# Block compression in a decoder layer: row-pair sums in place on VectorE and split a step later, a shorter GELU, weight splits at another spacing

## The chip, the cores and the metric

The kernel runs on one core of one Trainium2 chip. Its engines are TensorE (PE, and PEld for its weight loads), VectorE (DVE), ScalarE (ACT), GpSimd (POOL) and SyncE (SP), which issues most of the DMAs. The metric is the device time of one execution in microseconds, as the median of several runs; lower is better.

## The reference, cut to what matters

One decoder layer for a prompt of 256 tokens and for 8 sequences of 8 new tokens with 2048 cached tokens each: a SwiGLU block, a token mixer, a second SwiGLU block, each with a layer norm behind it. The mixer has a branch that compresses the cached keys and values. That is the part around the change:

```python
def compress(x, pos_emb, w1, w2):          # x: cached k or v, 16 tokens to a chunk
    chunks = x.reshape(B, n_chunks, CMP_STRIDE, NSA_KV_HEADS, NSA_HD)
    w1r = w1.reshape(2, CMP_STRIDE, NSA_HD, CMP_HIDDEN)
    h = einsum('pd,pdf->f', pos_emb, w1)
    for r in range(2):
        h = h + einsum('bnskd,sdf->bnkf', chunks, w1r[r])[:, r:r + n_cmp]
    return einsum('bnkf,fd->bnkd', gelu(h), w2)
```

Everything is float32. The kernel gets float32 precision from TensorE by splitting each operand into two numbers of a shorter type, a high part (a rounded copy) and a low part (the difference), and adding three products of parts.

## The kernel before

The program is written out in order: a Python generator emits one instruction stream per engine, each engine runs its stream in that order, and nothing is reordered afterwards. Background tasks (`spawn`) are woven in by a planner's clock: every matmul adds its estimated time to the clock, a task's `yield 2.5` means that its next part is emitted once 2.5 us more of matmuls have been emitted. So a yield decides beside which matmul an instruction stands, not when it runs.

The stages are: first SwiGLU, compression of the cache (`compress`), projections, attention, retention, output projection, second SwiGLU. Only the compression is touched.

**The compression** has 8 pairs (4 pairs of sequences for the keys, 4 for the values) and each pair 8 steps `m`, so 64 steps, and two halves `s2` in each step (`n` counts the 128 halves). In one half TensorE does three parts of six matmuls: two parts on even and odd rows (`eo`, weights `cw`) and a third on the sums of row pairs (`both`, weights `cs`). All are 128x128 by 128x256, 36 in a step. The operands of a step are made two steps ahead by `cx_split(m + 2)`: GpSimd adds the row pairs into two tiles `t` (L714), then ScalarE and VectorE split all rows (128x1024, into `r`) and the two sums (128x256 each, into `r` or `K`). `split` is L219 (ScalarE copies the high part) and L220 (VectorE subtracts it). Each buffer ring has three slots. The rows come in as 32 pages to a half of a pair by `cx_load` (L609); three rooms (`x0`, `x1`, `raw`) hold them in turn, and of each eight page loads SyncE issues six and GpSimd two.

When a pair's matmuls are done, `cpost` makes the output of the branch from them, twice (`f` 0 and 1): it puts the three accumulators together (L829 to L835), squares and adds the bias on ScalarE, runs `gelu` (L810, L811 on VectorE, the tanh on ScalarE at L813, L815 on VectorE), and then multiplies by `w2` on TensorE, at L208 into bank `m`. That product stands in TensorE's own stream between the matmuls of the next pair, so that TensorE waits there if L815 is late. After `f` 1, ScalarE copies the result to `y` (L852 or L855) and GpSimd stores it to `c_aside` (L858). From half 49 on, the weights of the value side are loaded and split while the key side is finished: `cw_split`, a half later the sum on GpSimd (`cw_sum`, L668) and `cs_split`.

Towards the end `x_scale` normalises the layer's input that was put aside, and `x_parts` splits it (L539, L540) for the first sweep of the projections. The tiles that it writes first lie in the memory where pair 6 keeps `y`, so they wait for pair 6's store to `c_aside`.

Of the kernel before, what the change touches and what calls it, by code (L numbers as in the profile page):

```python
# [11 lines left out]
AF = mybir.ActivationFunctionType  # L12
ALU = mybir.AluOpType
# [4 lines left out]
NT = 320  # L18
# [7 lines left out]
NTMP = 5  # L26
# [141 lines left out]
class Builder:  # L168
# [535 lines left out]

    def cx_split(self, m):
        half, j = divmod(m, 4)
        room = self.rooms[self.ROOMS[half]]
        x = room.rearrange("p (g a f) -> p g a f", g=32, a=4)[:, :, j]
        rows = x.rearrange("p g (s r c) -> p s r g c", s=2, r=2)
        eo, both = self.cx_ring(m)  # L710
        sums = []
        for s in range(2):
            t = self.t([128, NT], "t", bufs=NTMP)[:, 0:256]
            self.nc.gpsimd.tensor_tensor(t.rearrange("p (g c) -> p g c", c=8), rows[:, s, 0], rows[:, s, 1], op=ALU.add)  # L714
            sums.append(t)
        view = lambda t: t.rearrange("p (q g c) -> p g q c", q=4, c=8)
        self.split(view(eo[0]), view(eo[1]), x.rearrange("p g (q c) -> p g q c", c=8))
        for s in range(2):
            c = slice(256 * s, 256 * s + 256)
            self.split(both[0][:, c], both[1][:, c], sums[s])  # L720

    def compress(self):
# [7 lines left out]
        for n in range(128):  # L730
            m, s2 = divmod(n, 2)
            pair, i = divmod(m, 8)
            if s2 == 0:
                if n == 0:
                    self.rr_rest()
                if m < 62:
                    self.cx_split(m + 2)
                    self.rows_split = m == 61
                for load in loads.get(m, ()):
                    self.cx_load(*load)  # L740
# [29 lines left out]
            k, step = divmod(n - 49, 3)  # L770
            if 0 <= k < 8 and step == 0:

                self.cw_split(k, raw[k])
            elif 0 <= k < 8 and step == 1:
# [10 lines left out]
            if n == 114:  # L785
                self.w_limit, self.ahead = len(self.wq), 0
                self.w_feed()
# [19 lines left out]
    def gelu(self, hs, u, wait=0.0):  # L807

        nc = self.nc
        nc.vector.tensor_scalar(u, u, 0.044715, 1.0, op0=ALU.mult, op1=ALU.add)  # L810
        nc.vector.tensor_tensor(u, u, hs, op=ALU.mult)  # L811
        yield wait
        nc.scalar.activation(u, u, AF.Tanh, scale=math.sqrt(2.0 / math.pi))  # L813
# [3 lines left out]
    def cpost(self, pair, acc):  # L817
# [9 lines left out]
        for f in range(2):  # L827
# [16 lines left out]
            yield 2.5  # L844
# [920 lines left out]
    def first_splits(self, i):  # L1765
        self.cx_split(i)
        self.cs_split(i, self.sums_room(i))
# [117 lines left out]
```

## Time and profile before

| | us |
|---|---|
| median of 3 runs | 2862.51 |
| lowest, highest | 2862.44, 2864.89 |
| the profiled execution | 2862.96 |
| its span, first to last instruction | 2861.3 |
| TensorE busy in the span | 2786.0 (97%) |
| VectorE, ScalarE, GpSimd busy | 1580.3, 1210.4, 464.9 |
| compression: first matmul to the first of the projections | 947.48 to 1263.50 |

Times are microseconds from the span's start. A busy share of an engine is a mean over stages; the rows of the compression tell what each engine does there. Matmuls are pipelined: the distance of their starts is their cost, not the duration of one.

### The profile page before, as it was taken

To read this page: it belongs to the slowest core of one execution; us is meant where nothing else is said; L and a number is where in the kernel's file an instruction comes from. 1 tells how busy PE (TensorE), PEld (TensorE's weight loads), DVE (VectorE), ACT (ScalarE), POOL (GpSimd) and SP (SyncE) were. 2 spreads that over 40 slices of the span, in tenths; PEclk is the share of its full clock that TensorE was granted. 3 is DMA by queue.
4 is the path that set the end of the run, shared out by engine and by line. 5 is a ranking of instruction groups with operands and counts; after the bars stand their busy time and mean duration, and the time that the engine had idled before them with its cause. 6 is when DMAs were issued, how large, how long until landed. Compare 5 with 4: busy or idle time off the path is not lost. (4 is left out here: it accounts for less than half of the span.)

```text
span 2861.3 us, 49912 instructions
## 1 busy us (share of the span) xinstructions
PE 2786.0 (97%) x19841; PEld 2708.4 (95%) x19841; DVE 1580.3 (55%) x1939; ACT 1210.4 (42%) x1748; POOL 464.9 (16%) x548
## 2 busy tenths in 40 slices
PE   9999999999999998999999999999999999999996
PEld 8999999999999987998888888989999999999996
DVE  4333333347767878784574455673333333366665
ACT  4333333345445545554444445343333333354553
POOL 0000000000112656633232111450000000001111
PEclk9999999999999999999999999999999999999998
DMA  6555444455657444437677764544444444444442
GB/s 220 183 193 181 148 150 152 148 162 192 201 171 232 141 133 137 137 134 257 200 237 232 233 208 165 199 145 150 149 151 151 148 151 151 148 147 148 150 153 89
DMA packets 202603, 484.76 MB, mean 169 GB/s; under 512 B 24257, under 2 KB 100930, under 8 KB 200450
## 3 DMA queue, kind: packets, MB, share of 16 engines
q1 hardware_dynamic: 192546, 451.30, 49.1%
q0 software_dynamic: 9824, 30.29, 3.1%
q8 instruction: 155, 2.54, 0.4%
q14 instruction: 78, 0.64, 0.1%
HBM read 467.47 MB, written 22.28 MB: 171 GB/s over the span
## 5 line engine op out<-in xcount | busy, mean ns | idle before, releaser
L220 DVE TENSOR_TENSOR wl<-raw,wh 128x1024 fp32r<-128x1024 f32 x650 | 815.5, 1255 | 1066.4 <-ACT wh L219 1050.6
L219 ACT ACTIVATE wh<-raw 128x1024 fp32r<-128x1024 f32 x650 | 688.2, 1059 | 1153.2 <-PE m L214 1116.4
L213 PE MATMUL m<-x,wh 128*128 128x320 f32 x3664 | 1148.2, 313 | 9.1 <-ACT wh L219 6.5
L214 PE MATMUL m<-x,wh 128*128 128x320 f32 x3664 | 1132.4, 309 | 3.1 <-DVE x L540 3.1
L215 PE MATMUL m<-x,wl 128*128 128x320 f32 x3664 | 1132.0, 309 | 0.4 <-DVE wl L220 0.4
L213 PEld LDWEIGHTS m<-x,wh 128*128 128x128 f32 x3664 | 690.5, 188 | 32.3 <-issue 22.2
L214 PEld LDWEIGHTS m<-x,wh 128*128 128x128 f32 x3664 | 690.6, 188 | 5.1 <-DVE x L540 4.3
L215 PEld LDWEIGHTS m<-x,wl 128*128 128x128 f32 x3664 | 689.9, 188 | 0.8 <-DVE wl L220 0.8
L213 PE MATMUL m<-r,wh 128*128 128x320 f32 (+1 forms) x1592 | 495.4, 311 | 2.3 <-ACT wh L219 1.0
L215 PE MATMUL m<-r,wl 128*128 128x320 f32 (+1 forms) x1592 | 491.0, 308 | 0.0
L214 PE MATMUL m<-r,wh 128*128 128x320 f32 (+1 forms) x1592 | 487.8, 306 | 2.7 <-DVE r L220 2.7
L213 PEld LDWEIGHTS m<-r,wh 128*128 128x128 f32 x1592 | 298.8, 188 | 8.1 <-issue 3.7
L214 PEld LDWEIGHTS m<-r,wh 128*128 128x128 f32 x1592 | 299.3, 188 | 4.8 <-DVE r L220 3.9
L215 PEld LDWEIGHTS m<-r,wl 128*128 128x128 f32 x1592 | 298.5, 188 | 0.0
L476 POOL TENSOR_TENSOR t<-x,x 128x320 f32<-128x320 f32 x3 | 2.7, 916 | 1415.5 <-DVE x L456 719.6
L220 DVE TENSOR_TENSOR r<-G,r 128x640 fp32r<-128x640 f32 (+1 forms) x184 | 158.4, 865 | 0.0
L213 PE MATMUL x<-r,G 128*128 128x256 f32 x480 | 138.1, 288 | 0.0
L214 PE MATMUL x<-r,G 128*128 128x256 f32 x480 | 135.8, 283 | 1.4 <-DVE r L220 1.3
L215 PE MATMUL x<-r,G 128*128 128x256 f32 x480 | 135.1, 282 | 0.0
L219 ACT ACTIVATE r<-G 128x640 fp32r<-128x640 f32 (+1 forms) x184 | 130.1, 712 | 0.0
L214 PEld LDWEIGHTS x<-r,G 128*128 128x128 f32 x480 | 91.4, 190 | 3.4 <-DVE r L220 2.0
L213 PEld LDWEIGHTS x<-r,G 128*128 128x128 f32 x480 | 91.9, 192 | 1.4 <-issue 1.2
(389 smaller groups left out, 2390.3 us busy)
## 6 DMA issues: line engine op xcount, KB each, us to landing
raw<-wup SPq DMA_DIRECT2D x352, 512.0 KB
raw<-wdn SPq DMA_DIRECT2D x176, 512.0 KB
raw<-win_ret SPq DMA_DIRECT2D x48, 512.0 KB
raw<-win_nsa SPq DMA_DIRECT2D x40, 512.0 KB
raw<-wout SPq DMA_DIRECT2D x32, 512.0 KB
r<-pks SPq DMA_DIRECT2D x96, 128.0 KB
x<-pkc SPq DMA_DIRECT2D x152, 64.0 KB
K<-cw1k SPq DMA_DIRECT2D x16, 512.0 KB
```

The costliest lines, as they stand in the source:

```text
L213: mm(out, wh, xh, start=start, stop=False)
L214: mm(out, wh, xl, start=False, stop=False)
L215: mm(out, wl, xh, start=False, stop=stop)
L219: self.nc.scalar.activation(hi, src, AF.Copy)
L220: self.nc.vector.tensor_tensor(lo, src, hi.bitcast(F32), op=ALU.subtract)
L476: nc.gpsimd.tensor_tensor(s, self.d[0], self.d[1], op=ALU.add)
```

## The change

Four edits, all in the compression. Row pairs are no longer added by GpSimd into tiles of their own: VectorE adds both pairs in one instruction, in place in the room. Their split is one of 128x512 instead of two of 128x256 and is emitted one step later (`cx_both(m + 1)` beside `cx_split(m + 2)`). `gelu` has one VectorE instruction less: the first two are one. The weight splits of the value side stand 3.5 halves apart instead of 3, and the product with `w2` stands 5.0 planned us behind the GELU instead of 2.5 for pairs 0 to 6.

```diff
+    def cx_rows(self, m):
+        half, j = divmod(m, 4)
+        return self.rooms[self.ROOMS[half]].rearrange("p (g a f) -> p g a f", g=32, a=4)[:, :, j]
     def cx_split(self, m):
-        sums = []
-        for s in range(2):
-            t = self.t([128, NT], "t", bufs=NTMP)[:, 0:256]
-            self.nc.gpsimd.tensor_tensor(t.rearrange("p (g c) -> p g c", c=8), rows[:, s, 0], rows[:, s, 1], op=ALU.add)
-            sums.append(t)
+        x = self.cx_rows(m)
+        eo, _ = self.cx_ring(m)
         view = lambda t: t.rearrange("p (q g c) -> p g q c", q=4, c=8)
         self.split(view(eo[0]), view(eo[1]), x.rearrange("p g (q c) -> p g q c", c=8))
-        for s in range(2):
-            c = slice(256 * s, 256 * s + 256)
-            self.split(both[0][:, c], both[1][:, c], sums[s])
+        r = x.rearrange("p g (s r c) -> p g s r c", s=2, r=2)
+        self.nc.vector.tensor_tensor(r[:, :, :, 0], r[:, :, :, 0], r[:, :, :, 1], op=ALU.add)
+    def cx_both(self, m):
+        r = self.cx_rows(m).rearrange("p g (s r c) -> p g s r c", s=2, r=2)[:, :, :, 0]
+        _, both = self.cx_ring(m)
+        view = lambda t: t.rearrange("p (s g c) -> p g s c", s=2, c=8)
+        self.split(view(both[0]), view(both[1]), r)
...
                 if m < 62:
                     self.cx_split(m + 2)
-                    self.rows_split = m == 61
+                if m < 63:
+                    self.cx_both(m + 1)
+                    self.rows_split = m == 62
...
-            k, step = divmod(n - 49, 3)
-            if 0 <= k < 8 and step == 0:
+            k, step = divmod(2 * (n - 50), 7)
+            if 0 <= k < 8 and step in (0, 1):
                 self.cw_split(k, raw[k])
-            elif 0 <= k < 8 and step == 1:
+            elif 0 <= k < 8 and step in (2, 3):
...
-            if n == 114:
+            if n == 116:
                 self.w_limit, self.ahead = len(self.wq), 0
...
     def gelu(self, hs, u, wait=0.0):
-        nc.vector.tensor_scalar(u, u, 0.044715, 1.0, op0=ALU.mult, op1=ALU.add)
-        nc.vector.tensor_tensor(u, u, hs, op=ALU.mult)
+        nc.vector.scalar_tensor_tensor(u, u, 1.0 / 0.044715, hs, op0=ALU.add, op1=ALU.mult)
         yield wait
-        nc.scalar.activation(u, u, AF.Tanh, scale=math.sqrt(2.0 / math.pi))
+        nc.scalar.activation(u, u, AF.Tanh, scale=0.044715 * math.sqrt(2.0 / math.pi))
...
             yield from self.gelu(y, u, 1.5)
-            yield 2.5
+            yield 5.0 if pair < 7 else 2.5
...
     def first_splits(self, i):
         self.cx_split(i)
+        if i:
+            self.cx_both(0)
         self.cs_split(i, self.sums_room(i))
```

Two places show what moved. The first is VectorE's stream at the start of the compression, around the last four results of the first SwiGLU (L456). `r_856` and `r_867` (`r_865` after) are the rows of steps 0 and 1, `r_857` the sums of step 0, then of step 1, `wh` and `wl` hold weights. Before:

```order
L220 TENSOR_TENSOR r_856_8779<-x_791_7886,r_856_8779 128x32x4x8
L220 TENSOR_TENSOR r_857_8780<-t_8781,r_857_8780 128x256
L220 TENSOR_TENSOR r_857_8780<-t_8783,r_857_8780 128x256
L220 TENSOR_TENSOR wh_860_8791<-K_543_5515,wh_860_8791 128x512
L456 TENSOR_TENSOR x_587_5691<-x_587_5691,m_792_7887 128x320
L456 TENSOR_TENSOR x_589_5702<-x_589_5702,m_793_7894 128x320
L456 TENSOR_TENSOR x_591_5712<-x_591_5712,m_794_7901 128x320
L456 TENSOR_TENSOR x_593_5722<-x_593_5722,m_795_7908 128x320
L220 TENSOR_TENSOR r_867_8842<-x_791_7886,r_867_8842 128x32x4x8
L220 TENSOR_TENSOR r_857_8780<-t_8843,r_857_8780 128x256
```

After:

```order
L220 TENSOR_TENSOR r_856_8779<-x_791_7886,r_856_8779 128x32x4x8
L716 TENSOR_TENSOR x_791_7886<-x_791_7886 128x32x2x8
L220 TENSOR_TENSOR wh_858_8784<-K_543_5515,wh_858_8784 128x512
L456 TENSOR_TENSOR x_587_5691<-x_587_5691,m_792_7887 128x320
L456 TENSOR_TENSOR x_589_5702<-x_589_5702,m_793_7894 128x320
L456 TENSOR_TENSOR x_591_5712<-x_591_5712,m_794_7901 128x320
L456 TENSOR_TENSOR x_593_5722<-x_593_5722,m_795_7908 128x320
L220 TENSOR_TENSOR r_865_8835<-x_791_7886,r_865_8835 128x32x4x8
L716 TENSOR_TENSOR x_791_7886<-x_791_7886 128x32x2x8
L220 TENSOR_TENSOR r_857_8780<-x_791_7886,r_857_8780 128x32x2x8
```

L716 is the new sum in place. The split of step 0's sums, which stood ahead of the four results, now stands behind step 1's row split and sum.

The second is TensorE's stream where the compression ends: `x_1027` (`x_909` after) is the last accumulator of pair 7, `L208` the product of pair 6 with `w2`, and `m_1068` (`m_940` after) the first accumulator of the projections. Before:

```order
L214 MATMUL x_1026_13179<-r_856_8779,G_855_8752 128x256
L215 MATMUL x_1026_13179<-r_856_8779,G_855_8752 128x256
L213 MATMUL x_1027_13180<-r_857_8780,x_896_9287 128x256
L214 MATMUL x_1027_13180<-r_857_8780,x_896_9287 128x256
L215 MATMUL x_1027_13180<-r_857_8780,x_896_9287 128x256
L213 MATMUL x_1027_13180<-r_857_8780,x_896_9287 128x256
L214 MATMUL x_1027_13180<-r_857_8780,x_896_9287 128x256
L215 MATMUL x_1027_13180<-r_857_8780,x_896_9287 128x256
L213 MATMUL m_1068_13640<-x_1051_13560,wh_1042_13374 128x320
```

After:

```order
L214 MATMUL x_908_12870<-r_856_8779,G_855_8752 128x256
L215 MATMUL x_908_12870<-r_856_8779,G_855_8752 128x256
L208 MATMUL m_910_12878<-cw2v_384,x_872_8853 128x128 x4
L213 MATMUL x_909_12871<-r_857_8780,x_882_9250 128x256
L214 MATMUL x_909_12871<-r_857_8780,x_882_9250 128x256
L215 MATMUL x_909_12871<-r_857_8780,x_882_9250 128x256
L213 MATMUL x_909_12871<-r_857_8780,x_882_9250 128x256
L214 MATMUL x_909_12871<-r_857_8780,x_882_9250 128x256
L215 MATMUL x_909_12871<-r_857_8780,x_882_9250 128x256
L213 MATMUL m_940_13300<-x_932_13282,wh_917_13043 128x320
```

Pair 6's last product stands 6 matmuls ahead of the projections, where 54 matmuls stood between them before. In the same way every pair's first product stands 24 matmuls later than before, and every second one 48.

## Rows read from the trace of the kernel before

**Rows 1.** Page: busy us, share of the span and instructions of each engine.

```profile
PE 2786.0 (97%) x19841; PEld 2708.4 (95%) x19841; DVE 1580.3 (55%) x1939; ACT 1210.4 (42%) x1748; POOL 464.9 (16%) x548
```

**Rows 2.** Waits of PE, 947 to 1264: us in total, times, longest.

```profile
PE m L208 <- DVE x L815: 21.2, 6, 7.8
PE x L214 <- DVE r L220: 1.3, 2, 1.0
```

**Rows 3.** Timeline of PE: start, duration, instruction, [idle before <- releaser].

```profile
947.48 0.52 PE L213 MATMUL x<-r,G 128*128 128x256 f32 x1
...
1079.23 1.10 PE L208 MATMUL m<-x,cw2k 128*128 128x512 f32 x2 [1.83 <-DVE x L815]
...
1128.84 2.04 PE L208 MATMUL m<-x,cw2k 128*128 128x512 f32 x2 [7.78 <-DVE x L815]
...
1202.54 1.10 PE L208 MATMUL m<-cw2v,x 128*128 128x128 f32 x8
...
1238.04 1.09 PE L208 MATMUL m<-cw2v,x 128*128 128x128 f32 x8
...
1254.57 1.86 PE L208 MATMUL m<-cw2v,x 128*128 128x128 f32 x8 [2.21 <-DVE x L815]
...
1263.50 0.31 PE L213 MATMUL m<-x,wh 128*128 128x320 f32 x1
```

**Rows 4.** Windows: stretch, length, PE busy, granted clock, DMA share, GB/s.

```profile
1079.00:1083.00 4.00, 3.77 (x27) 1.00 0.19 56
...
1255.00:1259.00 4.00, 4.00 (x23) 0.59 0.36 103
```

**Rows 5.** Timeline of DVE, instructions beside which GpSimd added nothing.

```profile
948.87 1.23 DVE L220 TENSOR_TENSOR r<-x,r 128x1024 fp32r<-128x1024 f32 x1 [1.54 <-ACT r L219]
950.01 0.76 DVE L220 TENSOR_TENSOR r<-t,r 128x256 fp32r<-128x256 f32 x2
...
951.84 0.68 DVE L220 TENSOR_TENSOR wh<-K,wh 128x512 fp32r<-128x512 f32 x1
...
993.50 0.42 DVE L810 TENSOR_SCALAR x<-x 128x512 f32<-128x512 f32 x1
994.02 0.69 DVE L811 TENSOR_TENSOR x<-x 128x512 f32<-128x512 f32 x1
```

**Rows 6.** DVE by line and shape, 1057 to 1137: busy, mean ns of one.

```profile
L220 DVE TENSOR_TENSOR r<-t,r 128x256 fp32r<-128x256 f32 x18 | 15.1, 880 | 0.0
L220 DVE TENSOR_TENSOR r<-x,r 128x1024 fp32r<-128x1024 f32 x10 | 14.6, 1460 | 3.2 <-ACT r L219 3.2
L220 DVE TENSOR_TENSOR G<-K,G 128x1024 fp32r<-128x1024 f32 x8 | 11.0, 1381 | 3.4 <-ACT G L219 3.4
L220 DVE TENSOR_TENSOR K<-t,K 128x256 fp32r<-128x256 f32 x8 | 5.7, 750 | 0.0
L220 DVE TENSOR_TENSOR r<-raw,r 128x1024 fp32r<-128x1024 f32 x4 | 5.4, 1348 | 0.0
...
L220 DVE TENSOR_TENSOR wh<-K,wh 128x512 fp32r<-128x512 f32 x3 | 3.7, 1227 | 0.0
```

**Rows 7.** Timelines of POOL, ACT and PE: two sums; the late pages at 1018.

```profile
1134.84 1.43 POOL L714 TENSOR_TENSOR t<-x 128x256 f32<-128x256 f32 x2
...
1018.54 1.06 ACT L219 ACTIVATE r<-x 128x1024 fp32r<-128x1024 f32 x1 [9.63 <-DMA x<-pkc]
...
1021.16 0.39 PE L214 MATMUL x<-r,G 128*128 128x256 f32 x1 [0.39 <-DVE r L220]
```

**Rows 8.** Timelines of ACT, POOL and DVE at the end of the compression.

```profile
1256.47 0.60 ACT L855 ACTIVATE x<-m 128x512 f32<-128x512 f32 x1 [4.54 <-PE m L208]
...
1257.37 0.57 POOL L858 DMA_DIRECT2D c_aside<-x  x1 [12.92 <-ACT x L855]
...
1260.87 1.02 ACT L539 ACTIVATE x<-x,vecs 128x320 fp32r<-128x320 f32 x2 [3.80 <-DMA c_aside<-x]
...
1261.47 0.55 DVE L540 SCALAR_TENSOR_TENSOR x<-x,vecs,x 128x320 fp32r<-128x320 f32 x1 [4.49 <-ACT x L539]
```

More of the change, by code (lines that the diff above doesn't have):

```diff
@@ L703, in cx_ring @@
             [self.rb[m % 3][:, 512 * k:512 * k + 512] for k in range(2)]
+    def cx_rows(self, m):
+        half, j = divmod(m, 4)
+        return self.rooms[self.ROOMS[half]].rearrange("p (g a f) -> p g a f", g=32, a=4)[:, :, j]
     def cx_split(self, m):
[L706 to L710, printed above, removed]
-        sums = []
-        for s in range(2):
-            t = self.t([128, NT], "t", bufs=NTMP)[:, 0:256]
-            self.nc.gpsimd.tensor_tensor(t.rearrange("p (g c) -> p g c", c=8), rows[:, s, 0], rows[:, s, 1], op=ALU.add)
-            sums.append(t)
+        x = self.cx_rows(m)
+        eo, _ = self.cx_ring(m)
         view = lambda t: t.rearrange("p (q g c) -> p g q c", q=4, c=8)
         self.split(view(eo[0]), view(eo[1]), x.rearrange("p g (q c) -> p g q c", c=8))
-        for s in range(2):
-            c = slice(256 * s, 256 * s + 256)
-            self.split(both[0][:, c], both[1][:, c], sums[s])
+        r = x.rearrange("p g (s r c) -> p g s r c", s=2, r=2)
[5 more added lines that the diff above has]
+        self.split(view(both[0]), view(both[1]), r)
     def compress(self):
```

## Prediction

> **What bounds the kernel now.** I read the page's busy shares first: TensorE is busy for 97% of the span, the next engine, VectorE, for 55% [rows 1]. Over the whole span only TensorE can be the bound, so a change to other engines is worth what TensorE waits for in the stage that is touched. The waits of TensorE in the compression are next: 21.2 us in six waits of the `w2` product for L815, the last VectorE instruction of GELU, and 1.3 us for row splits [rows 2]. The starts of these products then give a ruler. Between 1202.54 and 1238.04 nothing waits: a pair of 8 steps costs 35.5 us, a step 4.44 us and one matmul 35.5 us less two products, over 288, about 0.117 us [rows 3]. Eight such pairs from 947.48 would end at 1231.5. The first matmul of the projections starts at 1263.50 [rows 3], so the stage holds 32 us that are not matmuls. 22.5 of them are the waits; most of the rest is the low clock behind the waits: after the one of 2.21 us the granted clock was 0.59 of 2.4 GHz (a stretch partly at its 1.2 GHz level) for 4 us, which costs 1.6 us, after the one of 1.83 us it stayed at 1.00 [rows 3, 4]. These **32 us are all that the change can win**.
>
> Why is L815 late? In the crowded stretch from 1057 to 1137, where weights are split as well, a step's rows cost VectorE 14.6 + 5.4 us in 14 instructions and the sums 15.1 + 5.7 us in 26, that is 1.43 + 2 x 0.80 = 3.03 us [rows 6]. Without GpSimd beside it the same work takes 1.23 + 0.76 = 1.99 us [rows 5]. So 1.04 us in a step is paid for the two sums that GpSimd makes at the same time; they take it 1.43 us [rows 7].
>
> **The change part by part.**
>
> *The sums move to VectorE.* Per step GpSimd loses two sums, VectorE gains one of 128x512. No such instruction is in the trace. From below it is bounded by a plain two-operand instruction of this size, 0.69 us, from above by one of this size with GpSimd beside it, 1.23 us [rows 5, 6]; I take 0.69, since GpSimd now adds only for the weights. The split is one of 0.68 us instead of two of 0.38 [rows 5]. A step's rows are then 1.23 + 0.69 + 0.68 + 0.1 for the sum's wait for the split in front of it (L811 starts 0.52 us behind L810, which lasts 0.42 [rows 5]) = 2.7 us: 0.3 us less than the crowded 3.03, but 0.7 more than the quiet 1.99. VectorE is not relieved much; it becomes independent of GpSimd.
>
> The Trainium skill (SBUF — State Buffer, section Who interferes with whom) says that a VectorE instruction with two SBUF inputs and a GpSimd instruction that reads SBUF exclude each other for their whole length. By that rule the two sums would have cost VectorE up to 1.43 us a step where the rows say 1.04, and the crowded stretch would lose 0.4 us x 18 steps = 7 us more of VectorE work than I count; the stalls that I leave there below would then be nil. The trace agrees in kind and is smaller in size; the sum goes by the rows.
>
> *GELU loses an instruction* of 0.42 us [rows 5], and its product with `w2` stands 24 (f 0) or 48 (f 1) matmuls later, 2.8 or 5.6 us. The shown waits: 1.83 goes with that alone; 7.78 needs 5 us more, and TensorE's own wait and VectorE's contention in front of L815 supply most of it; the 2.21 at the end goes too. I leave 1 us, which also covers pair 7, whose products stand 12 matmuls, 1.4 us, earlier. Bounds: 0, and 5 with the clock.
>
> *The sums are split a step later.* This is what the change costs, since TensorE's third part now follows its operands by one step less. In a quiet step they are ready in time: ScalarE 1.06 and, by size, 0.6, VectorE 2.7 us against a step of 4.44 plus two parts, 1.5 us. Three places are not quiet:
> - *Start.* The sums of step 0 were split ahead of 947; now they follow step 1's rows. VectorE starts these at 948.87 [rows 5]; 1.23 + 0.1 + 0.69 + 0.6 later the low part is there, at 951.4. TensorE wants it 13 matmuls behind 947.48, at 949.1. Cost 2.3 us; bounds 0 and 3.9 with the clock.
> - *Late pages at 1018.* ScalarE waits 9.63 us for pages until 1018.54, TensorE today only 0.39 us, because it lives on two finished steps [rows 7]. SyncE's page issues set that time, and they do not change. Now the sums of step 15 queue behind step 16's rows: 1.1 us of ScalarE, then 1.15 + 0.1 + 0.69 + 0.6 of VectorE, ready at 1022.2. Step 16's second matmul was due at 1020.8 [rows 7], and step 15's third part needs its low operand 24 matmuls ahead of that, at 1018.0, plus 1.4 us: the start's stall less the other 0.9 us of row waits, which go [rows 2, 7]. Cost 2.8, with 1 for the clock 3.8; bounds 1 and 5.
> - *The end.* `x_scale` and the last rows share VectorE; rows and GELU leave it 1 us a step, and no row prices the rest. I take half of the wait of 2.21 us that stands there now [rows 3], 1.2; bounds 0 and 4.
>
> *Crowded stretch.* The rows 2.7, the weights (1.23 + 0.68 quiet) / 1.75 steps = 1.1, and GELU with what stands before it, six instructions of 0.4 to 0.7 us twice in a pair less the 0.42 [rows 5], 0.7 a step: 4.5 us, less 0.08 for each start that overlaps the end in front of it, so about 4.1 against 4.44. GpSimd's weight sums still collide, and ScalarE still waits for them in its order. I keep 2.5 us for 14 steps; bounds 0 and 10 (the weights at the contended 1.38 and 1.23 of [rows 6], the sum's row at 0.9).
>
> *The store of pair 6.* The first sweep's operands may be written only when pair 6's result has been stored. Today the product starts at 1254.57, ScalarE copies it at 1256.47, GpSimd issues the store at 1257.37, ScalarE splits the first operand at 1260.87 and VectorE at 1261.47 [rows 3, 8]. That chain is 6.9 us long, 7.4 with VectorE's half, and 54 matmuls, 6.3 us, hid it: the projections start at 1263.50 without a wait. At full clock the product takes 1.1 instead of 1.86 us [rows 3], so the chain is 6.1 and 6.7 us. Now 6 matmuls stand between, and TensorE is through them 1.6 us after the product's start. **It waits some 5 us there**, 5.4 with the second operand, and pays 1.6 for the clock: 7.0 us. Bounds: 3 if the store lands faster, 9.
>
> *Nothing for:* the later weight release (n 116), since the first weights arrive ahead of the sweep; the spacing 3.5, counted above.
>
> Sum: 2.3 + 3.8 + 2.5 + 1.2 + 7.0 + 1 = 17.8 us of new stalls against 32 us that go. **14 us are left.** Its own time of the profiled execution is 2862.96 us, 1.7 more than the span and 0.45 above the median 2862.51, so 2862.5 - 13.5 to 14 gives 2849.
>
> **The rivals.**
> - *The small margins hold:* no stall at the start or in the crowded stretch, the store lands in 2 us. New stalls 8 us, time 2838 to 2841. For it: 0.6 us of the 4.44 are free. Against it: the wait at the store is plain in the order. Chance 0.18.
> - *The waits only move:* VectorE stays full in the crowded stretch, and what the `w2` product waited, the third part now waits, 10 us with the clock, and the late pages cost 5. New stalls 27 us, time 2857 to 2862. For it: 4.1 of 4.44 leaves little, and the bound above is 10. Chance 0.17.
> - *The edit does not do what it says:* the products still wait as now, since L815's lateness comes from ScalarE's order and not from VectorE. Then 10 of 22 us stay and 7 are added: 2858. Chance 0.04.
> - *VectorE becomes the bound of every step (slower):* the sum in place and its split read runs of 8 with gaps. At 1.23 us each they make 1.23 + 1.23 + 1.23 + 0.1, 3.8 us, with 0.7 of GELU 4.5 in every step; it decides from 4.44 on. In the 14 crowded steps 5.6 us, 16 us of stalls, elsewhere 0.1 x 50 = 5; with the 17.8 less 2.5, 36 us against 32: 2867, and 2890 if the row splits are dear too. Against it: the row split reads and writes such runs now, at 1.23 us for 1024, as much as a plain one. Chance 0.06.
>
> **How the numbers follow.** The forecast, 2849 (2843 to 2855), has 0.55; the others sum to 0.45. The range 2838 to 2862 holds the first rival, the forecast and the moved waits, and leaves out the slower case and the corners. What a measurement of this kernel can tell from no change is about 0.2%, 5.7 us: faster means below 2856.8. Faster: 0.55 + 0.18 + 0.03 of the moved waits = 0.76. Same: the rest of the moved waits and the fourth case, 0.16. Slower 0.08, where 0.02 stands for stalls at the store beyond my bound.
>
> **What would show it.** In the changed profile: no wait of the `w2` product above 2 us; a wait of 2 us of a third part for VectorE right behind the first matmuls, and one of about 3 near 1020; 4 to 6 us of idle TensorE between the last compression matmul and the first of the projections, ended by ScalarE's L539 and behind it the store to `c_aside`; L716 near 0.69 us; GpSimd busy about 100 us less. The forecast is wrong if L716 or the 128x512 split lasts over 1 us, if third parts wait in most steps, or if the projections start without a wait.

## The result and the profile after

| | before | changed |
|---|---|---|
| median, us | 2863.7 (4 runs beside the changed kernel) | 2882.3 (4 runs, 2879.4 to 2884.2) |
| profiled execution, its span | 2862.96, 2861.3 | 2884.2, 2882.5 |

The changed kernel is **slower**, by a ratio of 1.0054 (95% interval 1.0042 to 1.0066): 18.6 us between the medians, 12 to 19 us by the interval, where 14 us of gain were forecast. The page after, against [rows 1]:

```profile
span 2882.5 us, 49616 instructions
PE 2797.6 (97%) x19841; PEld 2715.4 (94%) x19841; DVE 1553.5 (54%) x1921; ACT 1202.3 (42%) x1684; POOL 346.5 (12%) x420
```

GpSimd is 118 us less busy and VectorE 27 us, as the edits mean it. Now TensorE's waits in the compression (us in total, times, longest), against [rows 2]:

```profile
PE m L214 <- DVE r L220: 10.1, 10, 2.8
PE m L214 <- DVE K L220: 4.5, 6, 1.7
PE m L213 <- ACT x L219: 3.4, 1, 3.4
PE x L214 <- DVE r L220: 2.5, 1, 2.5
PE m L213 <- ACT r L219: 2.4, 2, 1.3
```

No wait of the product with `w2` is left, and in their place third parts (into bank `m`, in pair 7 into `x`) wait for a split, 20 times in these rows. Single ones in TensorE's timeline of the changed kernel (start, us, line, what the idle time in brackets ended with), against [rows 3]: the start of the stage, pair 4's last step, a quiet pair, the first sweep of the projections, pair 7's product, and a later product that waits for a transfer.

```profile
951.66 0.48 PE L214 MATMUL m<-r,wh 128*128 128x256 f32 x1 [1.69 <-DVE r L220]
...
1151.32 0.39 PE L213 MATMUL m<-r,x 128*128 128x256 f32 x1 [3.38 <-ACT x L219]
...
1185.44 0.39 PE L214 MATMUL m<-r,K 128*128 128x256 f32 x1 [0.15 <-DVE r L220]
...
1274.67 0.42 PE L213 MATMUL m<-x,wh 128*128 128x320 f32 x1 [3.28 <-ACT x L539]
1275.69 0.41 PE L214 MATMUL m<-x,wh 128*128 128x320 f32 x1 [0.61 <-DVE x L540]
...
1317.50 0.74 PE L208 MATMUL x<-cw2v,r 128*128 128x128 f32 x4 [1.69 <-DVE r L819]
...
1329.90 0.67 PE L208 MATMUL x<-G,G 128*32 128x256 f32 x8 [1.66 <-DMA G<-cw1k]
```

The best reading is a ruler that counts work and not waits. The compression has 2304 matmuls beside the `w2` products, 288 to a pair. The table has the time from each pair's first matmul to the next one's (pair 7's to the first matmul of the projections), read from TensorE's timeline by counting. A pair without a wait takes 35.5 us; pair 0 has no product in it. The labels e1 to e18 are the experiments below; e15 to e17 also have the edge copy of e6 and the early product of e5.

| pair | 0 | 1 | 2 | 3 | 4 | 5 | 6 | 7 | sum |
|---|---|---|---|---|---|---|---|---|---|
| before | 37.4 | 35.6 | 42.6 | 43.4 | 46.2 | 35.7 | 35.5 | 39.6 | 316.0 |
| changed | 41.4 | 37.3 | 37.2 | 43.7 | 50.0 | 36.9 | 36.8 | 43.7 | 327.0 |
| e1 sums split at once | 38.9 | 43.4 | 39.5 | 52.0 | 58.9 | 40.0 | 38.5 | 48.0 | 359.2 |
| e2 sums on GpSimd, a step later | 41.2 | 39.4 | 35.5 | 46.1 | 51.1 | 35.7 | 35.6 | 41.4 | 326.0 |
| e3 changed, sums ahead of rows | 38.4 | 40.7 | 36.8 | 42.8 | 50.9 | 35.7 | 35.6 | 45.1 | 326.0 |
| e4 before, GELU and later product | 37.4 | 41.2 | 36.7 | 46.1 | 45.8 | 35.7 | 36.0 | 39.9 | 318.8 |
| e10 before, fixed pages | 37.5 | 35.5 | 36.1 | 43.5 | 46.2 | 36.6 | 35.5 | 38.1 | 308.9 |
| e13 before, no sums | 36.1 | 35.7 | 36.8 | 37.4 | 42.7 | 35.7 | 35.5 | 35.6 | 295.5 |
| e14 before, no weights | 37.4 | 35.7 | 43.1 | 35.4 | 35.4 | 35.7 | 35.5 | 38.2 | 296.4 |
| e17 new weights' order, rows first | 39.9 | 43.4 | 37.0 | 41.8 | 45.0 | 36.7 | 37.0 | 40.7 | 321.5 |
| e15 the same, sums ahead | 38.4 | 40.6 | 36.9 | 40.7 | 42.9 | 35.7 | 35.6 | 40.1 | 311.0 |
| e16 the same, early product | 38.4 | 35.4 | 37.8 | 39.1 | 44.2 | 35.7 | 35.5 | 36.3 | 302.4 |
| e18 without the new weights' order | 38.4 | 35.6 | 38.3 | 39.3 | 44.8 | 35.7 | 35.5 | 36.3 | 303.8 |

Of the 21.2 us between the two spans, 11 lie in the compression, 7.6 between the first sweep and the first product with the selected pages (147.4 us before, 155.0 after), and 2.4 behind it, less than the 4.8 us by which the changed kernel's own runs differ. The compression's loss is in pairs 0, 3 and 4, 5 and 6 and 7; pairs 1 and 2 gain 3.7 us. Eight pairs of 35.5 us would be 284: of the changed kernel's 43 us above that, 28.4 are idle time of TensorE (22.6 of 32 before), and the rest are matmuls at a slower pace behind waits, in part at a granted clock of 0.60 of 2.4 GHz (952 to 956) and 0.57 (1098 to 1102), stretches partly at the 1.2 GHz level.

What bounds pairs 3 and 4? Two windows, before and changed, over these pairs (bounds, length, then busy us of TensorE, its loads, VectorE, ScalarE, GpSimd, then granted clock and DMA):

```profile
1063.00:1153.00 90.00, 75.64 (x590) 71.64 (x589) 77.85 (x90) 50.67 (x87) 61.95 (x76) 0.94 0.46 134
```

```profile
1064.00:1157.00 93.00, 78.24 (x581) 73.35 (x581) 67.26 (x84) 47.46 (x71) 30.54 (x42) 0.94 0.47 136
```

VectorE fell from 86% busy to 72%, and the stretch became longer. No engine is full in it. What ScalarE and then VectorE wait for there, in the changed kernel:

```profile
ACT x L836 <- DVE x L835: 11.0, 4, 4.2
ACT wl L219 <- POOL K L668: 9.2, 3, 4.1
ACT wh L219 <- POOL K L668: 7.8, 3, 3.0
ACT x L219 <- POOL K L668: 5.0, 1, 5.0
```

```profile
DVE r L220 <- ACT r L219: 7.4, 9, 2.2
DVE G L220 <- ACT G L219: 5.7, 4, 2.6
DVE wl L220 <- ACT wl L219: 4.0, 2, 2.1
```

Each engine stands in its own order behind a wait for another one. What TensorE feels of that depends on the **lead** of its operands. I took, for each step, the start of its first matmul less the end of VectorE's row split for it. Before, the lead is 6.2 to 7.6 us in pair 6 and sinks to 1.9 at step 30 and -0.3 at step 35, and TensorE does not wait for rows there. In the changed kernel it never sinks under 4.1 and stands at 4.1 to 4.3 at twelve steps, 3, 6, 15, 23, 30, 35, 37, 47, 55, 58, 59 and 63: about a step (36 matmuls, 4.2 us) is now the least it can be, since the sums of step m queue behind the rows of step m+1, and TensorE must stop for them first. So late rows show as waits of the third part, a step earlier.

### The profile page after: what moved, and what is told of

Same layout as the page of the kernel before. It is cut to its first block, busy times and chain, and to the rows that moved or that the text cites. A ratio compares the mean times of both kernels' runs of the same rounds, so it can differ in the third digit from the quotient of the medians.

```text
span 2882.5 us, 49616 instructions
## 1 busy us (share of the span) xinstructions
PE 2797.6 (97%) x19841; PEld 2715.4 (94%) x19841; DVE 1553.5 (54%) x1921; ACT 1202.3 (42%) x1684; POOL 346.5 (12%) x420
## 5 line engine op out<-in xcount | busy, mean ns | idle before, releaser
L213 PEld LDWEIGHTS m<-x,wh 128*128 128x128 f32 x3664 | 692.0, 189 | 36.1 <-issue 22.6
L220 DVE TENSOR_TENSOR r<-x,r 128x1024 fp32r<-128x1024 f32 (+1 forms) x76 | 75.7, 996 | 40.3 <-ACT r L219 40.3
L213 PEld LDWEIGHTS x<-r,G 128*128 128x128 f32 x480 | 92.4, 192 | 1.1 <-issue 1.0
```

The costliest lines, as they stand in the source:

```text
L213: mm(out, wh, xh, start=start, stop=False)
L220: self.nc.vector.tensor_tensor(lo, src, hi.bitcast(F32), op=ALU.subtract)
```

## The experiments

All ratios are to runs of the kernel before on the same chip, with 95% intervals. Theory 1 was that the loss is the third part's lead, given up by the late split; its rival that VectorE's load, with the sum in it, makes everything late.

**e1: the split at once.**

```diff
                 if m < 62:
                     self.cx_split(m + 2)
-                if m < 63:
-                    self.cx_both(m + 1)
+                    self.cx_both(m + 2)
```

> The changed kernel with one thing undone: the sums in place are split at once, behind the row split of the same step (as the kernel before did), not a step later. VectorE still makes the sums. Theory 1 (the delay: the third part follows its operands by one step too little, and every lateness of VectorE or ScalarE now reaches TensorE): the 24 us of third-part waits between 947 and 1263 in the changed kernel go, the stall at pair 6's store and what follows it stay; 2852 to 2858. Theory 2 (VectorE's load: the sum of 0.69 to 1.0 us in its queue makes rows and GELU late, wherever the split stands): no more than a quarter of the waits goes; 2876 to 2884, with waits of first and second parts in place of third ones.

2910.6 us, 1.0156 (1.0139 to 1.0173): slower still. Neither theory had this. ScalarE's waits from 947 to 1063:

```profile
ACT r L219 <- DVE x L716: 20.7, 10, 2.1
ACT K L219 <- DVE x L716: 10.6, 5, 2.3
ACT r L219 <- DVE raw L716: 10.3, 5, 2.1
ACT K L219 <- DVE raw L716: 8.7, 3, 4.6
```

Directly behind the rows' high part ScalarE comes to the sums' high part, for which VectorE has first to finish the rows' low part and the sum: 50 us in 23 waits, as many as VectorE makes sums in that stretch, with all else on ScalarE queued behind. With the sum on VectorE some distance is needed; e3 and e15 show that it can be less than the changed kernel's.

**e2 and e3: whose load, which order.** e2 puts the sums back on GpSimd and leaves their split a step later:

```diff
-        self.nc.vector.tensor_tensor(r[:, :, :, 0], r[:, :, :, 0], r[:, :, :, 1], op=ALU.add)
+            self.nc.gpsimd.tensor_tensor(t..., rows[:, s, 0], rows[:, s, 1], op=ALU.add)
+            self.pair_sums[m % 3].append(t)
...
+            self.split(both[0][:, c], both[1][:, c], self.pair_sums[m % 3][s])
```

e3 exchanges two calls in the changed kernel:

```diff
-                if m < 62:
-                    self.cx_split(m + 2)
                 if m < 63:
                     self.cx_both(m + 1)
                     self.rows_split = m == 62
+                if m < 62:
+                    self.cx_split(m + 2)
```

> The changed kernel with the sums back on GpSimd (into tiles t, as before), but still split a step later, as two splits of 128x256. Theory 1 (the delay): third parts wait as in the changed kernel, 2876 to 2890, since ScalarE and VectorE still reach the sums behind the next step's rows. Theory 2 (VectorE's load): the third-part waits go with the sum, 2852 to 2862.

> The changed kernel with the order inside a step turned: the sums of step m+1 are split ahead of the rows of step m+2, not behind them. No instruction more or less. Theory 1 (the delay, by way of the queue: the sums wait in ScalarE's and VectorE's order behind 1.06 + 1.23 + 0.69 us of the next rows, and behind the pages that these wait for): most third-part waits and the start's go, rows have the slack, 2856 to 2866. Theory 2 (VectorE's load): the order changes nothing in the load, 2876 to 2886.

e2: 2879.1 us, 1.0044 (1.0027 to 1.0061); third parts wait as in the changed kernel, without any sum on VectorE. That speaks for theory 1. e3: 2875.9 us, 1.0035 (1.0022 to 1.0047), 5 to 6 us less than the changed kernel by ratio and median: the quiet pairs are mended and pair 0 in part (its first wait of 1.68 us stays), but pairs 1, 3 and 4 are not. Pairs 3 and 4 take 93.7 us in both. So the lead is a part of the loss only, and not, by itself, the loss of the crowded pairs.

**e4: the two edits that were to win, alone.** The kernel before with the shorter GELU and

```diff
-            yield 2.5
+            yield 5.0 if pair < 6 else 2.5
```

> The kernel before with only the shorter GELU and the later product with w2 (5.0 planned us instead of 2.5), for pairs 0 to 5. Sums on GpSimd, split at once, spacing 3. If the 22 us of w2 waits are lost only because the product stands too early: they go and nothing takes their place, as the third part keeps its two steps of slack: 2840 to 2846, waits of third parts under 2 us in sum. Rival (the waits only move: VectorE's lateness in the crowded stretch reaches the row splits instead): first or third parts wait 10 us or more, 2852 to 2860.

2867.4 us, 1.0008 (0.9997 to 1.0018): **nothing is won**, though no lead was given up for it. The waits of TensorE in the compression, and two rows of ScalarE's timeline:

```profile
PE m L208 <- DVE x L814: 18.3, 8, 4.5
PE x L214 <- DVE r L220: 3.1, 3, 1.2
```

```profile
1012.14 0.63 ACT L812 ACTIVATE x<-x 128x512 f32<-128x512 f32 x1 [1.95 <-DVE x L810]
1017.08 1.06 ACT L219 ACTIVATE r<-x 128x1024 fp32r<-128x1024 f32 x1 [4.31 <-DMA x<-pkc]
```

The product stands 24 or 48 matmuls later and waits 18.3 us in eight pieces, not 21.2 in six. `f` 1's GELU starts after `f` 0's product, so it moves with it; pair 0's second one came to wait 4.1 us behind the late pages of step 16. Pairs 1 and 2 are 77.9 us long (78.2 before), pairs 3 and 4 91.9 (89.6). The waits only moved, with the sums and their lead left alone. What they are the end of was the next question.

**e5: pair 6's product early** in the changed kernel.

```diff
-            yield 5.0 if pair < 7 else 2.5
+            yield 5.0 if pair < 6 else 2.5
```

> The changed kernel, but pair 6's product with w2 stands as early as before (2.5 planned us; the others stay at 5.0). Theory 1 (the store of pair 6 behind its late product holds the projections, and the low clock and the late start of pair 7 follow from it): the waits of 3.3 and 0.6 us at the first sweep go, the stage to the projections ends 5 to 6 us earlier and what is lost behind it shrinks too: 2872 to 2877. Theory 2 (the stall only moves to the product itself, since GELU of pair 6 is late anyway behind x_scale's VectorE work): a wait of 2 us or more at that product instead, 2878 to 2884.

2873.6 us, 1.0032 (1.0021 to 1.0044): 8.8 us less than the changed kernel by the medians, 6.3 by the ratios. The waits of 3.28 and 0.61 us at the first sweep shrink to 0.24 and 0.17, as the first theory had it. In the two profiles only some 2 us of the gain lie ahead of the first sweep, the rest behind.

**e6, e7, e8, e9: ScalarE's and GpSimd's waits.** e6 (before) and e8 (changed) put the small copy that ScalarE waits at (L832, L836) ahead of VectorE's sum. e7 and e9 are e6 with the weights' order changed: in e7 the split of the weights' sums stands half a step behind GpSimd's L668, in e9 L668 itself stands half a step later too, and the split behind that. The edge copy, and e9's weights:

```diff
             nc.scalar.activation(u[:, 0:256], q, AF.Copy)
+            nc.scalar.activation(rows[:, 1, 127:128], two(p[:, 254:256]), AF.Copy)
             yield 1.0
             nc.vector.tensor_tensor(rows[:, 1, 0:127], ...)
-            nc.scalar.activation(rows[:, 1, 127:128], two(p[:, 254:256]), AF.Copy)
...
+            if 0 < k < 9 and step == 0:
+                self.cs_split(k - 1, ...)
-            elif 0 <= k < 8 and step == 1:
-                self.cw_sum(place, r)
-                self.cs_split(k, place)
+            elif 0 <= k < 8 and step == 2:
+                self.cw_sum(..., raw[k])
```

> The kernel before with two lines exchanged: the small copy of the last column (L832, 128x2, ScalarE) stands directly behind the copy L829, ahead of VectorE's L831, and not behind it. Theory 3 (ScalarE stands in its order behind this copy, 22 us between 947 and 1160, with the rows' high parts queued behind it, so the length of the crowded pairs is a chain of ScalarE and VectorE waiting for each other and no engine's load): rows and tanh come earlier, the w2 waits fall by a third or more; 2850 to 2858. Rival (VectorE's load: it is busy for 78 of 90 us between 1063 and 1153): ScalarE's time there is idle anyway and the w2 waits stay; 2860 to 2867.

> As the one before, and the split of the weights' sums stands a half step behind GpSimd's sum, not directly behind it, so that ScalarE does not stand waiting for L668 (18 us between 1063 and 1160 in the kernel before). Theory 3: pairs 3 and 4, now 89.6 us long, shorten to 76 to 82; with the copy 2840 to 2852. Rival (VectorE's load): they stay at 87 to 92 us, 2858 to 2867.

> The changed kernel with the same two lines exchanged (its L835 and L836). Theory 3: ScalarE's 20 us at this copy go, rows reach the floor of the third part's slack less often; 2866 to 2876. Rival (VectorE's load, or the slack of the third part alone): 2878 to 2884.

> The kernel before with the two lines of the edge copy exchanged and the weight work of the value side pulled apart: GpSimd's sum L668 stands two half steps behind the weight split that it must wait for (one before), the split of these sums one half step behind it. Theory 3 (in the crowded pairs three engines stand in their order behind each other: VectorE's weight split, GpSimd's L668, GpSimd's row sums L714 behind it, ScalarE and VectorE behind those): GpSimd's 23 us of waits for VectorE in front of L668 go, and pairs 3 and 4 shorten from 89.6 to 75 to 82 us; 2844 to 2854. Rival (VectorE's own work, 78 of 90 us busy, sets them): 86 to 90 us, 2858 to 2866.

e6 2861.2 us, 0.9988 (0.9978 to 0.9997); e7 2862.7, 0.9987 (0.9977 to 0.9996); e8 2878.5, 1.0048 (1.0031 to 1.0064); e9 2862.9, 0.9996 (0.9987 to 1.0006). 3 or 4 us at most (e6), e8 not to be told from the changed kernel, and no more for taking GpSimd's waits away: theory 3 (engines that wait for each other in their orders, and no engine's load), as I had it, fell for the kernel before. In e9 VectorE is busy for 79 of the 86 us of pairs 3 and 4 and hardly waits; that its load, with GpSimd's sums beside it, is then the next limit is my reading, which e13 supports and no run isolates.

**e10: pages from fixed places** in the kernel before.

```diff
-                queue.dma_start(out=out, in_=self.I[name][bass.ds(v, 1)]...)
+                queue.dma_start(out=out, in_=self.I[name][(a + k + i) % 160][:, part])
```

> The kernel before, but the cached keys and values are taken from fixed pages and not from those in the page table (so the compression's input is another, and the reading of the table is left out); as many transfers of the same size by the same queues. SyncE issues pages almost without a pause from 960 to 1045 in the kernel before, 0.67 us each. Theory 4 (the page issues set when pair 2's rows come, and the w2 wait of 4.7 us at 1035 is ScalarE's wait for pages): an issue takes 0.35 to 0.45 us, ScalarE's wait of 9.6 us goes, pairs 0 to 2, now 115.6 us, shorten to 108 to 110, 2855 to 2859. Rival (the pages are early enough, GELU is late by itself): pair 2 stays at 42 us and the time at 2862 to 2866.

2859.7 us, 0.9985 (0.9975 to 0.9994), and pair 2 falls from 42.6 to 36.1 us. Of SyncE's timeline 24 page issues of the kernel before, then of e10:

```profile
984.04 15.86 SPq L609 DMA_DIRECT2D raw<-pkc  x24
```

```profile
979.81 11.24 SPq L607 DMA_DIRECT2D raw<-pkc  x24
```

And of TensorE's timeline pair 1's first product, in the kernel before, then in e10:

```profile
1040.12 1.19 PE L208 MATMUL m<-x,cw2k 128*128 128x512 f32 x1 [4.66 <-DVE x L815]
```

```profile
1034.96 0.67 PE L208 MATMUL m<-x,cw2k 128*128 128x512 f32 x1 [0.30 <-DVE x L819]
```

An issue takes 0.47 us in place of a mean of 0.66, pages come earlier, and the wait of 4.66 us "for L815" is gone. It was a wait for pages, by way of ScalarE's order.

**e11, e12: the spacing and the queue** in the changed kernel: weights 3 half steps apart; four of eight page loads on GpSimd in place of two.

```diff
-            k, step = divmod(2 * (n - 50), 7)
+            k, step = divmod(n - 49, 3)
```

```diff
-            self.pages(..., 2 if half > 1 else 0)
+            self.pages(..., 4 if half > 1 else 0)
```

> The changed kernel with the weight splits 3 half steps apart, as before. If the wider spacing costs (the last weight sum is needed at step 39, and TensorE waits 3.4 us there for its split): pair 4 falls from 50.0 to 45 or 46 us, 2876 to 2879. Rival (it is what keeps VectorE from being overrun, as the change means it): third parts wait more in pair 3, 2883 to 2890.

> The changed kernel, but GpSimd issues four of each eight page loads (two in the changed one): it has lost the row sums, 100 us of work, and SyncE is full from 960 to 1045. Theory 4 (SyncE's issues limit pairs 0 to 2): the third-part waits near 1018 and 1055 to 1060, 2.5 us with the clock's part 4, go; 2877 to 2880. Rival (the slack of the third part is short for its own reasons): 2881 to 2884.

e11: 2879.9 us, 1.0050 (1.0033 to 1.0067), not to be told from the changed kernel by the time; in the profile the wait of 3.4 us for the last weights at 1151.32 goes and pair 4 is 47.6 us long. e12: 2890.0 us, 1.0092 (1.0075 to 1.0109). My reading was wrong: GpSimd, in its order, now waits for rooms to come free with the weights' sums behind it, and ScalarE waits 6.1 us for one of these and 12.0 for three others (3.7 and 9.2 in the changed kernel). That accounts for a part of the loss only; pair 0 alone grew by 3.9 us, and I did not follow that up.

**e13, e14: without the sums, without the weights** in the kernel before.

```diff
-            self.nc.gpsimd.tensor_tensor(t..., rows[:, s, 0], rows[:, s, 1], op=ALU.add)
-            sums.append(t)
+            sums.append(rows[:, s, 0])
```

```diff
-            if 0 <= k < 8 and step == 0:
-                self.cw_split(k, raw[k])
-            elif 0 <= k < 8 and step == 1:
-                ...
```

> The kernel before with GpSimd's row sums left out: the third part is split straight from the first row of each pair (so its numbers are not the sums). Splits, their places and all else stay. It shows the most that taking the sums off GpSimd could win, as VectorE gets no sum in their place. If GpSimd's sums are what makes VectorE late in pairs 3 and 4 (its rows and splits are a third longer beside them): VectorE's busy time there falls from 78 to 60 us, the pairs from 89.6 to 76 to 80, the w2 waits of pairs 2 to 4 go, 2847 to 2853, with pair 2's wait for pages left. Rival (the weights' chain between ScalarE, VectorE and GpSimd sets the pairs): 85 to 90 us, 2858 to 2864.

> The kernel before with the value side's weights left out: no load, split or sum of them, the value side runs on the key side's weights (so its numbers are others). It shows what the weights cost in pairs 3 and 4. If these pairs are long only by the weight work: 71.5 to 73 us in place of 89.6, and only pair 2's wait for pages is left; 2844 to 2848. Rival (the row work alone already fills VectorE beside GpSimd's sums): 78 us or more, 2852 to 2858.

e13: 2849.6 us, 0.9942 (0.9925 to 0.9958); e14: 2848.7 us, 0.9942 (0.9926 to 0.9959). Pairs 3 and 4 take 80.1 us without the sums, 70.8 without the weights. So in the kernel before the weights make these pairs long; row work beside GpSimd's sums alone fits. The windows of e13 and e14 over the pairs:

```profile
1055.00:1135.00 80.00, 73.44 (x586) 70.40 (x585) 60.29 (x88) 49.65 (x87) 31.66 (x42) 0.96 0.55 158
```

```profile
1064.00:1135.00 71.00, 71.00 (x588) 69.08 (x588) 55.84 (x74) 38.83 (x71) 44.32 (x68) 1.00 0.44 125
```

VectorE's 77.85 us become 60.29, for the same splits and GELU work: 17.6 us in 16 steps are paid for GpSimd's sums. The sums' removal is worth 9.5 us there and 5.8 in pair 2, where the rows catch up faster once the pages are there; e13 keeps ScalarE's wait of 10.8 us for them.

**e15 to e18: can the change's idea win?** e15 is the changed kernel with the sums' split ahead of the rows (e3), pair 6's product early (e5), the edge copy first (e8) and the weights 3 half steps apart in the order of e9. e17 is e15 with the rows first again; e16 is e15 with all products at 2.5; e18 is e16 without the edge copy and the weights' order of e9. e18 against the changed kernel, beside e3's exchange:

```diff
-            yield 5.0 if pair < 7 else 2.5
+            yield 2.5
...
-            k, step = divmod(2 * (n - 50), 7)
+            k, step = divmod(n - 49, 3)
```

> The changed kernel with four things done otherwise: the sums of step m+1 split ahead of the rows of step m+2, pair 6's product early, the edge copy first, and the weights 3 half steps apart with GpSimd's sum two and its split three half steps behind the weight split. All work is done. If VectorE's shorter load (67 us in place of 78 in pairs 3 and 4) can be used once the third part's slack and the engines' orders are mended: pairs 3 and 4 take 78 to 84 us, no third part waits over 1.5 us, 2850 to 2858. Rival (the split behind the sum in place costs the slack anyway): 90 us or more, 2864 to 2872.

> As e15, but the product with w2 stands at 2.5 planned us in all pairs, as in the kernel before: of the changed kernel's four edits the later product is gone too. If the later product is of no use once VectorE is less busy (and in pair 1 harms, since GELU of pair 0 then queues behind the late pages: 3.5 us wait there in e15): pair 1 falls from 40.6 to 36 us and part of it returns in pair 2, 2851 to 2857. Rival (the later product is what keeps pairs 3 and 4 at 83.6 us): w2 waits there rise by 5 us or more, 2860 to 2866.

> As e15, but with the changed kernel's order inside a step: the sums of step m+1 split behind the rows of step m+2. It shows what the split's place alone costs. If the third part's lost slack is the main loss of the changed kernel: third parts wait 10 us or more again, pairs 5 and 6 take 36.8 in place of 35.7 us, 2866 to 2872. Rival (the weights' order and pair 6's product were the loss, and the place of the split is worth little): 2857 to 2861.

> The changed kernel with the sums in place and the shorter GELU, but the sums of step m+1 split ahead of the rows of step m+2, the product with w2 at 2.5 planned us everywhere and the weights 3 half steps apart; the edge copy and the weights' order as in the kernel before. If these three are enough (e16 without its edge copy and its weights pulled apart): 2853 to 2858, pairs 3 and 4 at 84 to 87 us. Rival (GpSimd's and ScalarE's waits at the weights hold the freed VectorE back, so that the sums alone gain nothing): pairs 3 and 4 at 90 us or more, 2860 to 2867.

| | us | ratio to before | interval |
|---|---|---|---|
| e15 | 2857.6 | 0.9968 | 0.9956 to 0.9981 |
| e17 | 2866.1 | 0.9999 | 0.9990 to 1.0008 |
| e16 | 2851.9 | 0.9949 | 0.9936 to 0.9963 |
| e18 | 2853.8 | 0.9964 | 0.9950 to 0.9977 |

The order inside a step costs 8.5 us (e17 less e15), the later product of pairs 0 to 5 another 5.7 (e15 less e16). The second number is less firm: the two intervals overlap, and of the 8.6 us by the ruler 5.2 are in pair 1 but 3.8 in pair 7, where the product of pair 6 stands at the same place in both. The sums in place and the shorter GELU, with neither and with the weights 3 half steps apart, win 10 to 14 us against the kernel before. e16 and e18 are faster than both kernels; the edge copy and the weights' order between them cannot be told apart by the time. e18 differs from the changed kernel in three placements alone and is 26 to 28 us faster: what the change lost, it lost by where instructions stand, not by the work it moved. In e18's pairs 3 and 4, 84.1 us long:

```profile
PE m L208 <- DVE x L819: 8.2, 3, 4.9
PE m L213 <- ACT r L219: 1.7, 1, 1.7
```

## Why the prediction was wrong

It forecast 2849 us, and the kernel takes 2882. By places, with the forecast's terms set against the ruler (my placing of the terms, made afterwards; the 1 us kept for GELU has no place in it):

| | before | forecast | measured |
|---|---|---|---|
| pair 0 (start, +2.3) | 37.4 | 39.7 | 41.4 |
| pairs 1 and 2 (waits go, late pages +3.8) | 78.2 | 74.9 | 74.5 |
| pairs 3 and 4 (waits go, crowded +2.5) | 89.6 | 73.6 | 93.7 |
| pairs 5 and 6 (nothing) | 71.2 | 71.2 | 73.7 |
| pair 7 to the projections (end +1.2, store +5.4) | 39.6 | 42.1 | 43.7 |
| projections to the selected pages (clock 1.6) | 147.4 | 149.0 | 155.0 |

**The step that failed first is the one from "all that the change can win" to "32 us that go".** 32 us is a fair upper bound. But the waits in it were put down to the product's place and to L815, the last releaser in the row, and so counted as gone once the product stands later. e4 does just that and wins nothing. 4.66 us of the 21.2 hung on SyncE's pages (e10), the 14.3 in pairs 3 and 4 on the weights' work (e14), about half of it with GpSimd's sums beside VectorE (e13). The 2.21 at the end is gone in e13 and 0.3 in e16 and e18, but 1.4 in e15; its cause stays open. A later product only lets another instruction reach such a wait first.

**The term that was most mis-sized is the crowded stretch: 2.5 us were left for it, and 22.6 were measured** (93.7 less two pairs of 35.5). The work was sized well: 4.1 us of VectorE in a step forecast, 67.26 / 16 = 4.2 measured. The inference from it was wrong: that work fits under the step does not mean that operands are in time, since VectorE waits for ScalarE and ScalarE for VectorE and GpSimd (the rows above). Of the 22.6 us, 9.6 go in e18 (84.1 us), with the sums split first, the product early and the weights 3 half steps apart. The order of the split alone is worth 0 to 3.2 of them (e3 against the changed kernel, e15 against e17), so the lost lead is the smaller part here. The other 13 stay in the best placement that was tried; e14, the kernel before without the weights' work, has none of them. Which of that work's waits they are, no run separates.

**"In a quiet step they are ready in time"** failed on a small scale: 1.3 us of waits in pairs 5 and 6 and 2.5 us of time, at the last two steps of each pair. e3 takes them away by the order alone, so this is the lost lead.

**GELU and the product**, with 1 us left over: no wait of a product is left, as forecast, but the later product wins nothing where nothing else is changed (e4) and costs some 5.7 us once the order is mended (e15 less e16). **The spacing**, counted at nothing of its own, let TensorE wait 3.4 us for the last weights (gone in e11, whose time cannot be told from the changed kernel's). The weight release at n 116 stands in every run made from the changed kernel, so its price isn't measured; e18, which keeps it, takes 148.5 us from the first sweep to the selected pages, 147.4 before.

**The late pages** look right in the table and are not. A wait of about 3 us near 1020 was forecast, behind pages that ScalarE waits for until 1018.5. In the changed kernel ScalarE waits for no page there but for GELU, ahead of step 16's rows, and two third parts wait 1.4 us together:

```profile
1018.29 0.63 ACT L817 ACTIVATE x<-x 128x512 f32<-128x512 f32 x1 [2.70 <-DVE x L815]
1019.03 1.06 ACT L219 ACTIVATE r<-x 128x1024 fp32r<-128x1024 f32 x1
```

```profile
1017.71 0.39 PE L214 MATMUL m<-K 128*128 128x256 f32 x1 [0.84 <-DVE K L220]
...
1022.73 0.39 PE L214 MATMUL m<-r,x 128*128 128x256 f32 x1 [0.56 <-DVE r L220]
```

That pairs 1 and 2 came to 74.5 us against 74.9 is luck: two more waits at 1055 and 1060, 1.1 us, which the forecast did not have, fill the sum up.

**The end**, 1.2 us, was too small: third parts of pair 7 wait 2.52 and 1.34 us for VectorE.

**Right in mechanism and near in size** were the start (1.69 us of wait, 2.4 to 4.0 us by the ruler in this profile and those of e5, e8 and e11, against 2.3) and pair 6's store: 3.28 + 0.61 us of wait against 5.4, and behind these waits a granted clock of 0.69 of 2.4 GHz, partly at the 1.2 GHz level, in the window's last number but two:

```profile
1277.00:1281.00 4.00, 4.00 (x22) 4.00 (x20) 4.00 (x7) 1.41 (x4) 2.28 (x2) 0.69 0.72 276
```

The wait came out shorter in part because from the store's issue to ScalarE's L539 it takes 2.39 us (1271.67 to 1274.06), and 3.50 in the kernel before. What hangs on it was left out. Pair 7's product waits 1.69 us, and a product waits 1.66 us for a transfer of a series that SyncE began 16.6 us later than before (1313.09 for 1296.53), where the sweep itself began 11.2 later. Early again, pair 6's product gives back 6.3 to 8.8 us, which does not tell from the 7 forecast. Why the projections still lose 5.9 us in e5, and hardly anything in e15, isn't settled; e5 shows one wait of 4.1 us for a transfer of that series.

**The rivals.** "The waits only move" is what happened, but I gave it 10 us in pairs 3 and 4, where it was 22.6, and thought of it as VectorE being full. The VectorE bound did not come. The mark set for it, over 1 us for L716 or the split, was met by three L716 alone; the groups of pairs 3 and 4 (busy us, mean ns, idle ahead) hide that in a mean:

```profile
L716 DVE TENSOR_TENSOR x<-x 128x512 f32<-128x512 f32 x12 | 10.2, 852 | 0.4
L220 DVE TENSOR_TENSOR r<-x,r 128x512 fp32r<-128x512 f32 x9 | 6.1, 682 | 0.0
```

Every other L716 takes 0.69 us. The three took 1.64, 2.11 and 1.66 us, each beside a sum of the weights on GpSimd (L668), as this one:

```profile
1095.59 1.64 DVE L716 TENSOR_TENSOR x<-x 128x512 f32<-128x512 f32 x1
```

```profile
1094.56 2.12 POOL L668 TENSOR_TENSOR K<-K 128x512 f32<-128x512 f32 x1 [6.58 <-issue]
```

The rule of the Trainium skill that I weighed (SBUF — State Buffer, Who interferes with whom) concerned how much VectorE pays for GpSimd's sums: e13 measures 17.6 / 16 = 1.1 us a step, near the 1.04 of the rows. That the stalls of the crowded stretch would be nil by the rule did not follow: VectorE was busy for 67.26 of 93 us there, and the stalls came all the same.

## What to carry to other kernels

A wait is named after its last link; before you count it as a gain, move that consumer alone and see whether the time falls, as here most of 21 us of waits for one instruction were pages and the weights' work. Operands made n steps ahead carry a lead that in-order engines spend on each other: read how low it sinks before giving up a step of it, since busy shares don't show that. When work moves to the engine that also feeds the next step, look where its consumer stands in every queue: here ahead of the next step's rows was best (e15), behind them cost 8.5 us (e17), and directly behind its producer cost most (e1).

## What the runs showed of the hardware that I had not expected

Beside GpSimd's sums, VectorE's instructions with two inputs from SBUF are held up for most of the sums' length: 1.1 us of 1.43 a step in the mean (e13). One split of the changed kernel, 1.23 us when alone (at 1281.85), beside two GpSimd additions:

```profile
1272.35 2.83 DVE L220 TENSOR_TENSOR wl<-raw,wh 128x1024 fp32r<-128x1024 f32 x1 [3.86 <-ACT wh L219]
```

```profile
1272.26 0.87 POOL L528 TENSOR_TENSOR x<-x,ln 128x320 f32<-128x320 f32 x1
...
1273.22 0.86 POOL L528 TENSOR_TENSOR x<-x,ln 128x320 f32<-128x320 f32 x1
```

1.23 + 0.87 + 0.86 is 2.96, against 2.83 measured: here the Trainium skill's rule (SBUF — State Buffer, Who interferes with whom), an exclusive lock on the ports that the two engines share, agrees with the row, where the mean of 1.1 us stays under it. GpSimd's page issues, which the changed kernel keeps, do not do this: VectorE's row split takes 1.22 us in its pairs 3 and 4, beside page issues too, against 1.46 [rows 6].

Reading a page's place from a table costs SyncE time of its own. In the kernel before six issues stand 0.53 us apart, and ahead of each six SyncE reads the next six places from the page table (L605; least, median and greatest ns between 960 and 1045):

```profile
L605 SPq TENSOR_LOAD <-pts x20: 714/722/732, 963.1 to 1042.4; - x20
```

That makes the mean of 0.66 us (24 in 15.86). From fixed places, in e10, they stand 0.47 us apart (24 in 11.24), and SyncE waits 25.3 us in six waits (950 to 1050) for rooms to come free. e10 leaves the reading out on GpSimd as well; with both, 6.5 us of pair 2's 7.1 us above 35.5 are gone.
